# Storing the output of a linear attention in pairs of octets instead of octet by octet

## The chip, the cores and the metric

The kernel runs on one core of one Trainium2 chip. The metric is the device time of the execution in microseconds (us); lower is better. A run's profile spans from its first to its last instruction, and that span is 1.7 to 2.2 us shorter than the time. Each run also reports the mean clock granted to TensorE. With one core there is no second die to compare with, so a run is called slow if it lies over 1.5% above the fastest run of the same kernel; all comparisons here use fast runs.

## The reference

```python
# Q, K, V: float32, batch 8, heads 12, sequence 512, dim 64
Q_feat, K_feat = np.maximum(0, Q), np.maximum(0, K)
KV = np.einsum('bhkd,bhkv->bhdv', K_feat, V)
K_sum = np.sum(K_feat, axis=2)
numerator = np.einsum('bhqd,bhdv->bhqv', Q_feat, KV)
denominator = np.einsum('bhqd,bhd->bhq', Q_feat, K_sum)
return numerator / (denominator[:, :, :, None] + 1e-10)
```

96 heads of 512 x 64 are 12.58 MB for each of Q, K, V and the output. The kernel works on octets of 8 heads (twelve of them, numbered 0 to 11); K and V come in groups of 4 heads (24 groups, two to an octet).

## The kernel before

The parts that the change and the argument touch. All loads are issued at the start, as far as buffers are free, and cast to bf16 on the way; a store of octet `o` waits on SyncE's queue behind a copy of 128 bytes out of K of a group loaded well ahead, the "gate", so that stores go out in step with the loads.

```python
qin, kin, vin = pool("qin", 7), pool("kin", 12), pool("vin", 12)
outp = pool("outp", DELAY + 2)                  # DELAY = 5
# ... load_kv(g) loads K and V of a group, load_q(o) Q of an octet, all on GpSimd's queue
def denom(o):                                   # 16 matmuls, then VectorE on 128x256
    # ... ps = the denominators of all pairs (head of a row, head)
    nc.vector.scalar_tensor_tensor(own, ps, 1e-10, mask_h, op0=Alu.add, op1=Alu.mult)
    nc.vector.tensor_reduce(out=den, in_=own, op=Alu.add, axis=mybir.AxisListType.X)
    nc.vector.reciprocal(rec[o], den)
def norm(o, j, ps, o_sb):                       # half an octet: 128x1024 f32 out of PSUM
    rs = slice(16 * j, 16 * j + 16)
    nc.vector.tensor_tensor(o_sb[:, rs], ps, rec[o][:, rs]..., op=Alu.mult)
def store(o, o_sb):
    if o + DELAY < NO:                          # the gate
        nc.sync.dma_start(out=scratch, in_=k_sb[2 * (o + DELAY)][0:1, 0, :])
    # ... octet 11 in two halves of 4 KB rows, the others whole: 8 KB rows
    nc.sync.dma_start(out=Ov, in_=o_sb)
# ... the end of the program
norm(o, 1, ps, o_sb)                            # o = 10
store(o, o_sb)
idle(5, o + 1)                                  # matmuls into a bank that nobody reads
out_t(o + 1, (0,)); denom(o + 1); out_t(o + 1, (1,))
idle(6, o + 1)
backs(o + 1)                                    # transpose back, norm, twice; then two stores
```

## Time and profile before

| | before |
|---|---|
| time, median of 4 runs | 126.73 us (126.48 to 126.86) |
| span of the profiled run | 124.8 us |
| mean granted TensorE clock | 0.949 |
| HBM traffic | 37.75 MB read, 12.58 MB written |
| last load packet ends / last store packet ends | 110.0 / 123.6 us |

The views that carry the argument about what bounds this kernel are in the prediction. Two more of the kernel before are needed later. The first is a table by stage of the tail: of the numbers behind each stretch, the last three are the granted clock, the busy share of the DMA engines (small overlaps can bring it above 1) and the GB/s as written, in which a load counts with its two bytes per element.

```profile
core 0: us, PE busy (x) PEld busy (x) DVE busy (x) ACT busy (x) POOL busy (x), PEclk, DMA share, GB/s
...
107.00:108.50 1.50, 1.10 (x18) 1.09 (x18) 1.43 (x5) 1.12 (x2) 0.00 (x0) 1.00 1.06 350
108.50:119.00 10.50, 8.40 (x100) 7.29 (x97) 8.03 (x15) 4.64 (x9) 0.00 (x0) 1.00 1.01 418
119.00:121.00 2.00, 0.00 (x0) 0.00 (x0) 0.57 (x1) 0.00 (x0) 0.00 (x0) 1.00 0.98 410
...
123.50:124.90 1.40, 0.00 (x0) 0.00 (x0) 0.00 (x0) 0.00 (x0) 0.00 (x0) 0.50 0.00 0
```

The DMA share stays at 0.98 to 1.06 up to 121 us: the loads end and the stores go on with no gap. After 123.5 us nothing moves any more.

The second is the record of completions. The trace has sixteen increments of a DMA's semaphore for every store. I read them as one from each of the 16 engines, when its own share has landed, so that they show how far apart the engines are; the rate of the last part of the changed kernel, below, agrees with this reading. In the kernel before they are 1.55 to 1.65 us apart for every store from 110 us on. The last store's begin at 122.36, their mean is 123.22, and the sixteenth comes at 123.91 us.

### The profile page before, as it was taken

What the parts mean: (1) busy time and instruction counts of PE and PEld (TensorE: products, weight loads), DVE (VectorE), ACT (ScalarE), POOL (GpSimd) and SP (SyncE); (2) the same over time, 40 slices, a digit from 0 to 9 for tenths busy, and PEclk for the clock granted to TensorE, in tenths of its full rate; (3) what the DMA queues carried; (4) which work ended last, traced back from release to release, by engine and by line L of the source; (5) the groups of instructions that cost most, each with busy time, mean ns of one, the idle gap of its engine ahead of it and who ended that gap; (6) DMA issues with size and microseconds to landing.
All of it is one profiled execution on the core that took longest, in us unless ns stands there. A gap on an engine that the chain in (4) does not pass through costs nothing.

```text
span 124.8 us, 2656 instructions
## 1 busy us (share of the span) xinstructions
PE 86.6 (69%) x1067; PEld 78.5 (63%) x1067; DVE 81.1 (65%) x176; ACT 79.4 (64%) x114; POOL 31.2 (25%) x62
## 2 busy tenths in 40 slices
PE   0032287998889899893598599399777577797600
PEld 0031285997878787792597499299576476695500
DVE  2257644759797997989147845934928918979430
ACT  0163369989898999988149558665939737737100
POOL 6902434314243331142133115034122000000000
PEclk9999999999999999999779859959999999999995
DMA  3999999999999999999999999999999999999993
GB/s 112 377 306 215 215 205 210 217 205 218 203 215 211 206 223 324 253 216 300 281 215 280 304 213 249 331 215 230 334 234 218 323 257 215 312 421 420 428 416 143
DMA packets 10748, 32.68 MB, mean 262 GB/s; under 512 B 1392, under 2 KB 1392, under 8 KB 9328
## 3 DMA queue, kind: packets, MB, share of 16 engines
q0 software_dynamic: 8064, 17.83, 74.7%
q1 hardware_dynamic: 2384, 13.63, 27.1%
q10 hardware_dynamic: 288, 1.05, 2.2%
q8 instruction: 8, 0.13, 0.4%
q14 instruction: 4, 0.03, 0.1%
HBM read 37.75 MB, written 12.58 MB: 403 GB/s over the span
## 4 chain that ended last, share of the span: by engine, by line
DMA 34%; DVE 30%; PE 23%; ACT 5%; issue 2%; DVEq 1%; SPq 0%; POOLq 0%; ACTq 0%
DMA v_sb<-in_V_dram 14%; DVE o_sb L234 13%; DMA q_sb<-in_Q_dram 13%; PE ps_kv L150 11%; DMA kv_first<-in_K_dram 7%; PE ps_bk L228 7%; DVE kf L136 5%; PE ps_qt L171 4%; DVE vo L138 3%; ACT kvd L160 2%; DVE vo L145 2%; PE ps_ot L201 2%; DVE den L218 2%; ACT qt L179 2%; DVE rec L222 1%
## 5 line engine op out<-in xcount | busy, mean ns | idle before, releaser
L150 PE MATMUL ps_kv<-vo,kf 128*128 128x132 bf16 x384 | 30.8, 244 | 17.7 <-ACT vo L143 8.2
L150 PEld LDWEIGHTS <-kf 128*128 128x128 bf16 x384 | 28.4, 110 | 19.0 <-DVE vo L138 10.9
L234 DVE TENSOR_TENSOR o_sb<-ps_bk,rec 128x1024 f32<-128x1024 f32 x24 | 28.3, 1219 | 17.1 <-PE ps_bk L228 17.1
L160 ACT CAST kvd<-ps_kv 64x260 bf16<-64x260 f32 (+1 forms) x54 | 18.7, 346 | 19.5 <-PE ps_kv L150 16.6
L203 ACT COPY ot_sb<-ps_ot 128x1024 f32<-128x1024 f32 x24 | 24.0, 1014 | 3.0 <-PE ps_ot L201 2.0
L179 ACT ACTIVATE qt<-ps_qt 128x1024 bf16<-128x1024 bf16 x23 | 22.4, 1026 | 5.6 <-PE ps_qt L171 5.5
L228 PE MATMUL ps_bk<-ident,ot_sb 128*128 128x128 f32 x192 | 23.0, 273 | 0.4 <-ACT ot_sb L203 0.4
L136 DVE TENSOR_SCALAR kf<-k_sb,mask 128x1024 bf16<-128x1024 bf16 x44 | 18.4, 460 | 6.4 <-DMA k_sb<-in_K_dram 6.3
L94 POOL DMA_DIRECT2D k_sb<-in_K_dram x22 | 11.9, 542 | 37.7 <-DMA q_sb<-in_Q_dram 24.1
L228 PEld LDWEIGHTS ps_bk<-ident,ot_sb 128*128 128x128 f32 x192 | 20.8, 141 | 0.7 <-ACT ot_sb L203 0.7
L171 PE MATMUL ps_qt<-ident,q_sb 128*128 128x128 bf16 x192 | 16.0, 250 | 6.0 <-DMA q_sb<-in_Q_dram 5.9
L171 PEld LDWEIGHTS <-q_sb 128*128 128x128 bf16 x192 | 14.3, 114 | 7.3 <-DMA q_sb<-in_Q_dram 7.1
L201 PE MATMUL ps_ot<-qt,kvd 128*128 128x256 bf16 x96 | 14.7, 283 | 5.0 <-DVE o_sb L234 4.3
L96 POOL DMA_DIRECT2D v_sb<-in_V_dram x22 | 12.3, 558 | 17.4 <-DMA k_sb<-in_K_dram 11.1
L201 PEld LDWEIGHTS <-kvd 128*128 128x128 bf16 x96 | 9.2, 101 | 7.8 <-issue 5.7
L138 DVE TENSOR_SCALAR vo<-v_sb,mask 128x1024 bf16<-128x1024 bf16 x22 | 10.6, 482 | 1.8 <-DMA v_sb<-in_V_dram 1.8
L143 ACT ACTIVATE vo<-v_sb,mask 128x1024 bf16<-128x1024 bf16 x10 | 11.5, 1152 | 0.2
L210 PEld LDWEIGHTS <-qt 128*128 128x128 bf16 x192 | 6.8, 97 | 4.4 <-ACT qt L179 3.4
L210 PE MATMUL ps_den<-kvd,qt 128*128 128x16 bf16 x192 | 7.5, 180 | 2.4 <-ACT qt L179 2.1
L100 POOL DMA_DIRECT2D q_sb<-in_Q_dram x12 | 6.6, 546 | 8.5 <-DMA v_sb<-in_V_dram 6.2
L213 DVE SCALAR_TENSOR_TENSOR own<-ps_den,mask_h 128x256 f32<-128x256 f32 x12 | 5.0, 417 | 3.3 <-PE ps_den L210 3.3
L136 DVE TENSOR_SCALAR kf<-kv_first,mask 128x1024 bf16<-128x1024 f32 x4 | 2.8, 749 | 5.1 <-DMA kv_first<-in_K_dram 5.1
(24 smaller groups left out, 28.3 us busy)
## 6 DMA issues: line engine op xcount, KB each, us to landing
out_dram<-o_sb SPq DMA_DIRECT2D x11, 1024.0 KB, 9.0
q_sb<-in_Q_dram POOLq DMA_DIRECT2D x12, 512.0 KB, 14.8
k_sb<-in_K_dram POOLq DMA_DIRECT2D x22, 256.0 KB, 14.1
v_sb<-in_V_dram POOLq DMA_DIRECT2D x22, 256.0 KB, 13.2
kv_first<-in_V_dram ACTq DMA_DIRECT2D x2, 512.0 KB, 7.2
kv_first<-in_K_dram SPq DMA_DIRECT2D x2, 512.0 KB, 6.9
out_dram<-o_sb SPq DMA_DIRECT2D x2, 512.0 KB, 4.3
scratch<-k_sb SPq DMA_DIRECT2D x7, 0.1 KB, 5.0
```

The lines of the kernel that those rows point to most:

```text
L96: nc.gpsimd.dma_start(out=v_sb[g].rearrange("p r d -> p (r d)"), in_=Vr[g])
L136: nc.vector.tensor_scalar(kf[g][:, :, s, :], k_sb[g], scalar1=0.0, scalar2=mask[:, 0, s:s + 1], op0=Alu.max, op1=Alu.mult)
L138: nc.vector.tensor_scalar(vo[g % NB][:, :, 0, 2:D + 2], v_sb[g], scalar1=mask[:, 1, 0:1], scalar2=None, op0=Alu.mult)
L150: nc.tensor.matmul(ps_kv[:, g % 2, 0:2 * (D + 2)].rearrange("p (t d) -> p t d", t=2), kf[g][:, r, :, :].rearrange("p s d -> p (s d)"), vo[ ...
L160: copy(kvd[o % NK][64 * c:64 * c + 64, 4 * gs.start + s:4 * gs.stop:2, c * D1:c * D1 + D1].rearrange("p (g t) d -> p g t d", t=2), ps_kv[6 ...
L171: nc.tensor.transpose(ps[:, u, :], q_sb[o][:, i * (U // 2) + u, :], ident)
L179: nc.scalar.activation(to, ps, Act.Relu)
L201: nc.tensor.matmul(ps[:, i], kvd[o % NK][:, h, 1:2 * D + 1], q[:, :, h, :], start=True, stop=True, skip_group_check=True)
L203: nc.scalar.copy(ot[o][:, :, 4 * j:4 * j + 4], ps.rearrange("p h u c -> p u h c"))
L210: nc.tensor.matmul(ps[:, u], qt_sb[o % NZ][:, u, :], kvd[o % NK][:, :, 0:2 * D1:2 * D1 - 1], start=True, stop=True, skip_group_check=True)
L228: nc.tensor.transpose(ps[:, 2 * v:2 * v + 2].rearrange("p c d -> p (c d)"), ot[o][:, 8 * j + v].rearrange("p h c -> p (h c)"), ident32)
L234: nc.vector.tensor_tensor(o_sb[:, rs], ps, rec[o][:, rs].unsqueeze(2).to_broadcast([P, 16, D]), op=Alu.mult)
```

## The change

The first eight octets are stored in pairs: four stores of 2.1 MB with rows of 16 KB instead of eight of 1.05 MB with 8 KB. To bring a pair's rows together, Q of the two octets is interleaved before the transposes back, and the denominators of a pair are formed on 128x512 at a time. Pairs lag one pair behind. The last four octets go octet by octet as before. Three gates remain of seven, and the fourth pair's is on V of the last group: that store is to wait until all of K and V is in. Load buffers shrink to pay for larger output tiles.

```diff
-    qin = pool("qin", 7)
-    kin = pool("kin", 12)
-    vin = pool("vin", 12)
+    qin = pool("qin", 6)
+    kin = pool("kin", 9)
+    vin = pool("vin", 9)
-    outp = pool("outp", DELAY + 2)
+    outp = pool("outp", 3)
# ... kvd, qt_sb, ps_den, rec hold a pair; denom(o, x, n) works on n = 16 or 8 heads
-    def store(o, o_sb):
-        if o + DELAY < NO:
-            nc.sync.dma_start(out=scratch, in_=k_sb[2 * (o + DELAY)][0:1, 0, :])
+    def store(a):
+        gate = (None, k_sb[14], k_sb[18], v_sb[23])[a]
+        if gate is not None:
+            nc.sync.dma_start(out=scratch, in_=gate[0:1, 0, :])
+        nc.sync.dma_start(out=Or2[a], in_=o_sb[a].rearrange("p r d -> p (r d)"))
# ... octets 0 to 7 paired; then, L = 8:
+    a = L // 2
+    kvs(L)
+    prep(2 * L + 2)
+    prep_v(2 * L + 2, nc.scalar)
+    backs(a - 1, (0, 1))
+    octet(L)
+    prep(2 * L + 3)
+    prep_v(2 * L + 3, nc.vector)
+    kvs(L + 1)
+    backs(a - 1, (2, 3))
+    store(a - 1)
+    qt(L + 1)
+    backs(a, (0, 1))
+    store_octet(L, 1)
# ... octets 9, 10, 11 in the order of before
```

## The prediction

> **What bounds the kernel now.** I read the page's slices and DMA queues first, then windows of single phases, then the stores' issues on SyncE's queue, then VectorE's timeline over the last octets. (An octet is 8 heads: 3.15 MB read, 1.05 MB written; there are twelve.)
>
> ```profile
> DMA  3999999999999999999999999999999999999993
> GB/s 112 377 306 215 215 205 210 217 205 218 203 215 211 206 223 324 253 216 300 281 215 280 304 213 249 331 215 230 334 234 218 323 257 215 312 421 420 428 416 143
> ...
> q0 software_dynamic: 8064, 17.83, 74.7%
> q1 hardware_dynamic: 2384, 13.63, 27.1%
> ...
> HBM read 37.75 MB, written 12.58 MB: 403 GB/s over the span
> ```
>
> The DMA row is full from the second slice to the last but one. Q0 carries the casting loads (17.83 MB landed in bf16, so twice that leaves HBM), q1 the stores and half of the first loads.
>
> ```profile
> core 0: us, PE busy (x) PEld busy (x) DVE busy (x) ACT busy (x) POOL busy (x), PEclk, DMA share, GB/s
> 21.00:42.00 21.00, 19.35 (x262) 17.95 (x261) 16.94 (x35) 18.88 (x27) 7.21 (x14) 1.00 1.10 211
> 47.30:51.00 3.70, 3.14 (x40) 2.50 (x39) 3.18 (x5) 3.50 (x7) 0.43 (x1) 1.00 1.03 338
> 103.00:107.00 4.00, 2.89 (x36) 2.29 (x35) 3.59 (x6) 3.00 (x4) 0.00 (x0) 1.00 1.13 216
> 110.00:119.00 9.00, 6.90 (x86) 5.79 (x84) 6.53 (x11) 3.59 (x5) 0.00 (x0) 1.00 1.01 423
> ```
>
> The last column counts bytes as written. With loads alone (21 to 42 us) 211 GB/s is 422 GB/s at HBM; stores alone (110 to 119) move 423. In a mix (47.3 to 51) 338 written means, if loads plus stores still make about 418 at HBM, 258 of stores and 160 of loads: a store takes almost two thirds while it runs. So one number serves all phases: 50.33 MB at 421 GB/s is 119.5 us; with about 2 us before the first data and 3 us for the last ramp and the end, that is the 124.8 us span. The measured time is 1.9 us above the span. Compute may be late by any amount that leaves DMA work queued, and no more.
>
> ```profile
> 42.90 0.59 SPq L242 DMA_DIRECT2D scratch<-k_sb  x1
> 43.53 0.57 SPq L249 DMA_DIRECT2D out_dram<-o_sb  x1
> ...
> 102.85 0.50 SPq L242 DMA_DIRECT2D scratch<-k_sb  x1
> 103.45 11.23 SPq L249 DMA_DIRECT2D out_dram<-o_sb  x5
> 118.47 1.46 SPq L247 DMA_DIRECT2D out_dram<-o_sb  x2
> ```
>
> A store is issued as its gate, a load four to five octets ahead, has landed: one every 10 us. From 103.45 on the stores come ungated; the last two halves of the last octet are issued at 118.5 and 119.6 (the two in the last line) and land 4.3 us later. In the packet records stores run without a gap through this; at 119.6 some 0.4 to 0.9 MB of older stores was still ahead of the last half. That is 1 to 2 us of slack: compute that ends later than that shows in the time.
>
> ```profile
> 86.23 2.35 DVE L234 TENSOR_TENSOR o_sb<-ps_bk,rec 128x1024 f32<-128x1024 f32 x2 [1.57 <-PE ps_bk L228]
> ...
> 90.77 0.48 DVE L145 TENSOR_SCALAR vo<-v_sb,mask 128x1024 bf16<-128x1024 bf16 x1
> 94.23 2.36 DVE L234 TENSOR_TENSOR o_sb<-ps_bk,rec 128x1024 f32<-128x1024 f32 x2 [2.97 <-PE ps_bk L228]
> ...
> 99.96 0.48 DVE L145 TENSOR_SCALAR vo<-v_sb,mask 128x1024 bf16<-128x1024 bf16 x1
> 103.41 2.35 DVE L234 TENSOR_TENSOR o_sb<-ps_bk,rec 128x1024 f32<-128x1024 f32 x2 [2.97 <-PE ps_bk L228]
> 105.69 0.48 DVE L136 TENSOR_SCALAR kf<-k_sb,mask 128x1024 bf16<-128x1024 bf16 x1
> ```
>
> This is the compute that ends last. Per octet VectorE waits for TensorE's transposes back (2.97 us twice), normalises (2.35 us), and prepares two groups. From 86.2 to 105.7 there is no wait for a load: the chain VectorE, TensorE, VectorE sets the pace, 9.2 us an octet. From preparing group 22 (105.69) to the last half's issue (119.6) it is 13.9 us.
>
> **What the Trainium skill says.** "DMA: Bandwidth & Descriptors", Bandwidth, gives a fabric ceiling of 435 GB/s and 425 measured for 16 MB; the 421 to 423 above agree, so at most some 3% is left whatever the row size. Its Rules for kernel authors ask for 1 MiB or more per DMA; the stores have that already. In Queues, rings and completion order it says that an engine goes round-robin between queues at packet granularity; the two-thirds share of the 8 KB store rows beside loads agrees in kind, and would let 16 KB rows take at least as much. "VectorE: DVE Perf Modes", Why PSUM operands drop a tier, caps fp32 from PSUM at 1x; the normalisation (1219 ns for 1024 elements) and the masked add (417 ns for 256) agree: 1.04 ns for each further element.
>
> **The change part by part.**
>
> *Bytes and packets.* The bytes are the same. Stores go from 13 to 9 and gate copies from 7 to 3. A completion packet takes some 20 ns on an engine and a gate's 8-byte packet 36 ns (packet records), so 4 x 20 + 4 x (36 + 20) = 0.3 us at best. An 8 KB store packet takes 317 ns (25.8 bytes per ns), a 4 KB one mostly 159 (also 25.8): no fixed cost per row is visible, so 16 KB rows should bring nothing. Sum: 0 to -0.3 us on the floor.
>
> *Load buffers 12 to 9, Q 7 to 6.* A load is issued about 14 us before it lands, and compute is at most two octets behind; 9 buffers are 4.5 octets, above 33 us. No stall: 0.
>
> *VectorE per pair.* The paired denominators run twice per pair on 128x512 instead of 128x256: the masked add 417 + 256 x 1.04 = 0.68 us, the reduction likewise 0.69. Per pair + 4 x 0.27 = 1.1 us. Work per octet goes from 6.9 to 7.5 us, but it is uneven: an even octet has two preparations and two normalisations (about 6.1 us with the wait for TensorE), an odd one has the same plus 2 x (0.68 + 0.69 + 0.35), and waits for denominators and transposes in turn: about 10.7 us. At the start the two clears of kvd are twice as long and two more reductions are made (2 x 0.49 + 2 x 0.28 = 1.5 us), while octet 0 loses its denominators (1.2 us). A pair is then some 16.8 us against 14.2 (7.1 an octet between 26.3 and 40.7 us). DMA gives a pair 15 us in the load-only phase and 20 with stores. So compute, in step with the loads before, becomes 2 to 4 us late around 48 us and recovers partly: I place the start of octet 8 at 83 to 85 us, where before it was held by q_sb to 80.8 and by the preparation to 82.
>
> *Pair stores.* 2.1 MB at two thirds to four fifths of the bandwidth is 6.3 to 7.5 us in which loads crawl, against 4 us for one octet. Q of octets 5, 7 and 9 lands 1 to 2.5 us later; the even octets' land as before. About 1 us of this joins the lateness, the rest hides.
>
> *The tail.* The fourth pair's four normalisations come in octets 8 and 9's time, because pairs run one behind: between the start of octet 8 and group 22 VectorE now has eight normalisations, where it had six. Two more are 2.44 us, with TensorE's 16 transposes (1.9 us) between them, on the chain of the last fence. By hand, in the program's order on each engine and with the durations above: second half of octet 8's preparation 84.8; transposes and normalisations of pair 3 to 89.4; denominators 90.6; preparation 92.2; rest of pair 3 to 96.75; octet 8's own to 99.7; preparation, denominators, preparation to 103.7; octet 9's normalisations 106.7 to 109.0. Group 22 is prepared at 107.5 to 109.5 instead of 105.7: +2 to +4 us. From there on the program is as before, so the last half is issued at about 122.5.
>
> *The reserve.* At the last V's landing (before: about 106.6; after: about the same) there wait q_sb of octet 11 and 6.3 MB of stores: 7.3 MB, 17.5 us, to 123.7. That would cover a chain that ends by about 121. At 122.5 the queue has run dry or nearly: the last half then needs about 3.5 us (latency, 1.25 us of data, completion) instead of 4.3. Sum: +3.0 (chain) - 0.8 (no queue) - 0.3 (fewer packets) = +1.9 us: 128.6.
>
> **The rivals.** First, DMA stays the bound: full reserve, compute ends in time, 126.2 to 126.9. For it speaks that the DMA row is full in every slice and the gate on the last V is meant for just this. Against it: only 1 to 2 us of slack, and two normalisations more on a chain without load waits. Second, the odd octets run longer than I think, or the pair stores starve the loads at four fifths: chain +5 to +6, 130.5 to 131.5. For it: every odd octet has five handovers between TensorE and VectorE; against it: from octet 4 on DMA leaves 20 us a pair, in which 18 would still fit. Third, 16 KB rows or fewer changes between reads and writes raise the rate: mixed phases at 418 against 423 leave 1% of 30 us, 0.3 us; the equal rate of 4 and 8 KB packets speaks against more. 126.0.
>
> **Range and chances.** DMA-bound 126.3 and chain-bound 128 to 130.5 make a lopsided range, 126.2 to 130.8. The 2% line is 129.27, that is +2.5 us, inside the likely spread of the chain (+1 to +4.5 after the queue's slack): slower 0.38. Faster would need 124.2, below what 50.33 MB at the ceiling of 435 GB/s allow with the same start and end (115.7 + 5 + 1.9 = 122.6 at a perfect rate, never seen here): 0.03.
>
> **What would show it.** The store-only rate stays 420 to 427 GB/s and 16 KB packets take about 635 ns; if they take less than 610, the third rival has something. VectorE's masked add at 128x512 shows 0.65 to 0.72 us; odd octets are 3 to 5 us longer than even ones. Q of octet 7 lands later than 70.8, that of octet 8 not. Group 22's preparation starts after 107; the last store is issued after 121, and the DMA row has a hole or a thin slice just before the end. If instead the last issue is before 121 and the DMA row is full to the end, the chain's lateness was absorbed and the time is within 0.5 us of before.

## The result and the profile after

The time is 128.07 us (median of 4 runs, 127.96 to 128.17) against 126.73. All ratios here are the mean time of one kernel's fast runs over the mean of the other's of the same rounds, so not quite the ratio of the medians quoted. This one is 1.0108, with a 95% interval of 1.009 to 1.0126: 1.1% slower, within the 2%. The span grew from 124.8 to 126.3 us, and the granted clock rose from 0.949 to 0.979.

Of the page of the changed kernel, the slices' DMA share and GB/s, the stores' queue q1, the larger of two queues of kind "instruction", and the rate:

```profile
DMA  3999999999999999999999999999999999999981
GB/s 100 384 309 210 217 204 211 212 209 220 202 216 210 206 215 337 389 238 214 211 213 350 388 225 215 209 208 309 364 294 212 212 208 204 370 423 407 425 354 40
...
q1 hardware_dynamic: 1680, 13.63, 26.3%
...
q8 instruction: 8, 0.13, 0.4%
...
HBM read 37.75 MB, written 12.58 MB: 398 GB/s over the span
```

The DMA row is full up to the end, as before, except that the end is longer: the last two slices show 8 and 1, with 354 and 40 GB/s. Such a row hides a short gap in the middle of a slice. The table by stage, with the stretches used for before, shows it:

```profile
107.00:108.50 1.50, 1.01 (x13) 0.76 (x10) 1.50 (x5) 0.83 (x1) 0.00 (x0) 1.00 0.83 254
108.50:119.00 10.50, 8.88 (x111) 8.01 (x111) 7.96 (x18) 5.74 (x11) 0.00 (x0) 1.00 1.00 416
119.00:121.00 2.00, 0.62 (x6) 0.38 (x4) 2.00 (x2) 0.00 (x0) 0.00 (x0) 1.00 0.79 328
...
123.50:124.90 1.40, 0.00 (x0) 0.00 (x0) 0.00 (x0) 0.00 (x0) 0.00 (x0) 0.83 0.06 23
```

There are three differences. Between 107.0 and 108.5 us the DMA share falls to 0.83 (before 1.06): a hole where the loads end. Between 119 and 121 it is 0.79 (before 0.98): a dry spot just before the last halves are issued. And after 123.5 us, where before nothing moved, 23 GB/s still do. In the packet records the hole costs 0.5 us of the average engine's time and the dry spot 0.3 to 0.4 us.

SyncE's queue shows where the hole comes from:

```profile
82.68 0.50 SPq L276 DMA_DIRECT2D scratch<-k_sb  x1
83.28 0.53 SPq L277 DMA_DIRECT2D out_dram<-o_sb  x1
106.31 0.50 SPq L276 DMA_DIRECT2D scratch<-v_sb  x1
106.90 0.65 SPq L277 DMA_DIRECT2D out_dram<-o_sb  x1
107.65 13.85 SPq L283 DMA_DIRECT2D out_dram<-o_sb  x5
```

The fourth pair's store hangs on the gate of the last V. That V lands at 106.3 us, the gate copy is issued then, the store behind it at 106.90, and its first data moves at 108.05 (packet records). Meanwhile only Q of octet 11 is left to load, and it ends on the first engine at 107.3 and on the last at 108.8 us. An engine that has finished has nothing to do until 108.05.

The tail of the DMA work is best seen in fifths of a microsecond. These are the GB/s from 119 to 127 us, of the kernel before and of the changed one:

```profile
GB/s 492 369 410 451 389 389 430 410 430 328 410 471 369 430 430 348 287 266 287 164 184 102 21 0 0 0 0 0 0 0 0 0 0 0 0 0 0 0 0 0
```

```profile
GB/s 246 614 328 369 532 410 328 123 0 328 451 369 430 410 328 492 389 389 389 471 389 389 82 20 20 20 41 20 20 0 0 0 0 0 0 0 0 0 41 0
```

Before, the rate falls off over 1.5 us, because the engines are that far apart. After, it stands at about 400 until 123.4 and then at 20 for 1.2 us: one engine of sixteen (421 / 16 is 26 GB/s) is alone. The completions say the same. For the last store, fifteen increments come between 123.79 and 123.95 us, and the sixteenth at 125.22.

VectorE's timeline answers to the compute shown of before:

```profile
86.05 2.35 DVE L263 TENSOR_TENSOR o_sb<-ps_bk,rec 128x1024 f32<-128x1024 f32 x2 [0.89 <-PE ps_bk L255]
...
93.15 2.35 DVE L263 TENSOR_TENSOR o_sb<-ps_bk,rec 128x1024 f32<-128x1024 f32 x2 [2.08 <-PE ps_bk L255]
95.79 2.35 DVE L263 TENSOR_TENSOR o_sb<-ps_bk,rec 128x1024 f32<-128x1024 f32 x2 [0.29 <-PE ps_bk L255]
...
104.97 2.35 DVE L263 TENSOR_TENSOR o_sb<-ps_bk,rec 128x1024 f32<-128x1024 f32 x2 [2.97 <-PE ps_bk L255]
107.25 0.87 DVE L142 TENSOR_SCALAR kf<-k_sb,mask 128x1024 bf16<-128x1024 bf16 x2
...
118.78 2.36 DVE L263 TENSOR_TENSOR o_sb<-ps_bk,rec 128x1024 f32<-128x1024 f32 x2 [1.64 <-PE ps_bk L255]
```

The eight normalisations between the start of octet 8 and group 22 are the first four of these lines, two in each. Group 22's preparation begins at 107.25 (before 105.69), and the last pair of normalisations at 118.78 (before 117.22): the compute is 1.56 us later.

### Where the sixteenth engine's lag comes from

Besides loads, stores and gates, the packet records have a few packets of the instruction queues. Q8 has eight packets of 16 KB in a run, each 0.89 to 0.97 us long, and from the first to the last one comes on average after every 257 (before) or 262 (after) instructions of TensorE: TensorE is fetching its program. A single packet can only be on one of the sixteen DMA engines; the records don't say on which. The Trainium skill, "Runtime: NRT & Kernel Launch", Instruction fetch mechanics, describes just this: the instruction memory is refilled in 16 KiB blocks of 256 instructions over a DMA queue, and the cost of a crossing is "mostly hidden". Size and distance agree with the trace; whether it is hidden is the question here. Four stores' sixteen completions, as time of the first and the lag of the second-last and the last behind it, with TensorE's last fetch at 111.7 us (before) and 114.6 us (after):

| | before: first, 15th, 16th | after: first, 15th, 16th |
|---|---|---|
| store that completes just before the fetch | 110.07, +1.47, +1.55 | 113.33, +0.29, +0.39 |
| the next | 112.51, +1.56, +1.64 | 115.81, +0.41, +2.11 |
| the last but one (first half of octet 11) | 121.13, +1.54, +1.55 | 122.48, +0.19, +1.52 |
| the last | 122.36, +1.53, +1.55 | 123.79, +0.16, +1.43 |

In the changed kernel the hole lines the engines up, since those that are ahead wait for the store and those behind do not; then, within the store that follows the fetch, one of them falls 1.7 us behind the fifteenth, more than the 0.9 us of the fetch's own packet, and it is still 1.3 us behind the fifteenth at the end. Before, the engines were 1.6 us apart already, and the fetch made no difference to the last of them. That is an observation on two traces; the experiments test it.

### The profile page after: what moved, and what is told of

Same layout as the page of the kernel before. It is cut to its first block, busy times and chain, and to the rows that moved or that the text cites. A ratio compares the mean times of both kernels' runs of the same rounds, so it can differ in the third digit from the quotient of the medians.

```text
span 126.3 us, 2613 instructions
## 1 busy us (share of the span) xinstructions
PE 82.8 (66%) x1067; PEld 75.5 (60%) x1067; DVE 86.4 (68%) x178; ACT 79.2 (63%) x114; POOL 31.9 (25%) x62
## 3 DMA queue, kind: packets, MB, share of 16 engines
q10 hardware_dynamic: 288, 1.05, 2.1%
## 4 chain that ended last, share of the span: by engine, by line
DVE 33%; PE 26%; DMA 20%; ACT 12%; issue 3%; DVEq 1%; SPq 0%; ACTq 0%
DVE o_sb L263 15%; DMA v_sb<-in_V_dram 13%; PE ps_kv L156 10%; PE ps_bk L255 9%; DMA kv_first<-in_K_dram 7%; DVE kf L142 4%; ACT kvd L167 4%; ACT qt L191 4%; PE ps_qt L178 3%; ACT ot_sb L222 3%; DVE den L244 3%; DVE own L236 2%; DVE vo L144 2%; PE ps_ot L220 2%; PE ps_den L232 2%
## 5 line engine op out<-in xcount | busy, mean ns | idle before, releaser
L156 PE MATMUL ps_kv<-vo,kf 128*128 128x132 bf16 x384 | 27.9, 232 | 21.7 <-ACT vo L149 8.2
L156 PEld LDWEIGHTS <-kf 128*128 128x128 bf16 x384 | 25.6, 103 | 22.8 <-DVE vo L144 10.8
L255 PE MATMUL ps_bk<-ident,ot_sb 128*128 128x128 f32 x192 | 23.6, 274 | 0.5 <-ACT ot_sb L222 0.5
L178 PE MATMUL ps_qt<-ident,q_sb 128*128 128x128 bf16 x192 | 14.2, 233 | 1.8 <-DMA q_sb<-in_Q_dram 1.8
L178 PEld LDWEIGHTS <-q_sb 128*128 128x128 bf16 x192 | 13.0, 106 | 2.6 <-DMA q_sb<-in_Q_dram 2.3
L232 PE MATMUL ps_den<-kvd,qt 128*128 128x32 bf16 (+1 forms) x192 | 8.7, 195 | 5.4 <-ACT kvd L167 4.5
L232 PEld LDWEIGHTS <-qt 128*128 128x128 bf16 x192 | 8.1, 100 | 6.8 <-issue 5.7
L236 DVE SCALAR_TENSOR_TENSOR own<-ps_den,mask_h 128x512 f32<-128x512 f32 (+1 forms) x12 | 6.9, 579 | 6.7 <-PE ps_den L232 6.7
L103 POOL DMA_DIRECT2D q_sb<-in_Q_dram x12 | 7.2, 601 | 8.2 <-DMA v_sb<-in_V_dram 4.5
L244 DVE TENSOR_REDUCE den<-own 128x32 f32<-128x512 f32 (+1 forms) x12 | 7.1, 595 | 0.3
```

The lines of the kernel that those rows point to most:

```text
L156: nc.tensor.matmul(ps_kv[:, g % 2, 0:2 * (D + 2)].rearrange("p (t d) -> p t d", t=2), kf[g][:, r, :, :].rearrange("p s d -> p (s d)"), vo[ ...
L178: nc.tensor.transpose(ps[:, u, :], q_sb[o][:, i * (U // 2) + u, :], ident)
L232: nc.tensor.matmul(ps[:, u], qt_sb[a % NZ][:, x * U + u, :], kvd[a % NK][:, h0:h0 + n, 0:2 * D1:2 * D1 - 1], start=True, stop=True, skip_g ...
L255: nc.tensor.transpose(ps[:, 2 * v:2 * v + 2].rearrange("p c d -> p (c d)"), ot[a][:, 8 * j + v], ident32)
```

## The experiments

Two theories of the +1.34 us: *the chain* (compute that ends later, as predicted; then moving the gate changes nothing, and more delay costs its full size) and *the gate* (the hole behind the last V; then undoing the gate alone brings the time back, with compute as late as it is; the texts call this the queue theory, and the straggler theory where the lagging engine is meant). For the second, it is also open whether the hole itself or the lagging engine makes the loss. Twelve kernels ran, each beside 11 runs of the kernel before on the same chip (medians 126.71 to 126.81).

**1 and 2. One and two more normalisations on the chain (changed kernel).** The second half of octet 9 is normalised two or three times, each 1.22 us of VectorE.

```diff
-    backs(a, (2, 3))
+    backs(a, (2,))
+    backs(a, (3,), 1)        # and 2: the normalisation once and twice more, same result
     store_octet(L + 1, 1)
```

> The changed kernel with octet 9's last normalisation done twice: the chain on VectorE becomes 1.2 us longer, the stores and bytes stay. Chain theory (as in the prediction: the end is set by VectorE's chain, 1.56 us later than before): 128.07 + 1.2 = 129.3 us. Queue theory (the end is set by the one of 16 DMA engines that is 1.3 us behind the others through all the last stores, because an instruction fetch of 0.93 us fell on it after a hole had lined the engines up): the other 15 engines take up the 1.2 us, 128.1 to 128.4 us.

> The same with the normalisation done three times, chain 2.4 us longer. Chain theory: 130.5 us. Queue theory: the 15 engines now end last, 2.4 us after the last issue: 129.2 to 129.5 us, that is a rise of 1.2 and not of 2.4.

Measured 130.29 us (128.88 to 130.49, 6 runs, ratio 1.0264, 1.0227 to 1.03) and 130.77 (130.66 to 131.46, 5 runs, 1.0336, 1.0313 to 1.0358). The first is more than either theory had, because more than 1.22 us was added. In its profiled run (129.93) the last pair of normalisations starts 2.36 us later than in the changed kernel (121.14 against 118.78), and nearly half of that arises at 81.7 us, far ahead of the edit. TensorE's groups there, of the changed kernel and of experiment 1, with the idle time ahead of them in brackets:

```profile
81.45 1.07 PE L178 MATMUL ps_qt<-ident,q_sb 128*128 128x128 bf16 x16 [0.98 <-DMA q_sb<-in_Q_dram]
82.36 1.11 PE L156 MATMUL ps_kv<-vo,kf 128*128 128x132 bf16 x16
```

```profile
81.68 1.65 PE L178 MATMUL ps_qt<-ident,q_sb 128*128 128x128 bf16 x16 [0.99 <-DMA q_sb<-in_Q_dram]
83.13 3.05 PE L156 MATMUL ps_kv<-vo,kf 128*128 128x132 bf16 x31
```

The same 16 transposes take 1.07 us in one and 1.65 in the other, after the same idle time of 1 us, and the granted clock over these stretches is 1.00 and 0.61. The kernel before has such a slow stretch there too (0.61 from 80.8 to 85.2 us). It comes and goes between runs of one kernel: the run of 128.88 us fits a chain without it. The Trainium skill, "TensorE: Matmul & The Clock Gate", Part 1, has a cold state at half clock after an idle window of about 3.4 us; here waits of 1.0 to 2.5 us came before such a stretch in some runs, and in the changed kernel none followed a wait of 1.0 us. So a delay of this kernel's compute is uncertain by 1.1 us in itself. What follows for the theories: in the changed kernel the end does follow a chain that is made later still. The fifteenth completion of the last store moves by the same 2.36 us (126.31 against 123.95), the run's time by 1.8, since the sixteenth is now 0.94 us behind instead of 1.27. That lag isn't the old one: in the store before it, the sixteen completions are within 0.18 us, and a packet of the other instruction queue falls at 125.5. In experiment 2's profiled run (130.69) the last pair starts 4.05 us later than in the changed kernel, not 2.44; the fifteenth completion moves by 4.01 (127.96), the sixteenth comes 0.03 us behind it, and the time moves by 2.6. So no slack is left there, but that doesn't make the chain the cause of the first 1.34 us.

**3. The gate of the fourth pair on the last K (changed kernel).**

```diff
-        gate = (None, k_sb[14], k_sb[18], v_sb[23])[a]
+        gate = (None, k_sb[14], k_sb[18], k_sb[23])[a]
```

> The changed kernel with the fourth pair's store gated on the last K instead of the last V, 1.2 us earlier. Queue theory: the hole between the last load and the fourth pair's store (rate down to 200 GB/s, 0.5 us lost per engine) closes; 127.5 to 127.7 us, and the engines stay spread. Chain theory: the chain is not touched, 128.0 to 128.2 us.

Measured 126.89 us (126.57 to 127.74, 6 runs), ratio 1.0031 (1.0002 to 1.0059). One word brings back 1.2 of the 1.34 us. The tail by stage, and its GB/s from 119 to 127 us:

```profile
107.00:108.50 1.50, 0.85 (x8) 0.60 (x7) 1.50 (x5) 1.00 (x2) 0.00 (x0) 1.00 1.09 388
...
119.00:121.00 2.00, 0.45 (x5) 0.21 (x2) 1.97 (x2) 0.00 (x0) 0.00 (x0) 1.00 0.55 227
...
123.50:124.90 1.40, 0.00 (x0) 0.00 (x0) 0.00 (x0) 0.00 (x0) 0.00 (x0) 0.50 0.00 0
GB/s 451 246 246 328 82 164 123 0 307 328 492 369 410 389 451 369 430 389 451 369 451 82 0 0 0 0 0 0 0 0 0 41 0 0 0 0 0 0 0 0
```

The hole is gone (1.09) although the compute is as late as in the changed kernel: the last pair of normalisations starts at 118.61 (118.78 there). The dry spot is deeper (0.55), since the same bytes went out earlier. It costs nothing: the last store ends at 123.90 us, as before (123.91), and its sixteen completions lie within 0.3 us. They were 2.0 us apart before the dry spot, so there the engine that lagged caught up. Two of the six runs took 127.74 us; they have no profile, and why is not known.

**4. The gate on K of group 22, where the kernel before has it (changed kernel).**

```diff
-        gate = (None, k_sb[14], k_sb[18], v_sb[23])[a]
+        gate = (None, k_sb[14], k_sb[18], k_sb[22])[a]
```

> The changed kernel with the fourth pair's gate on the K of group 22 (3.7 us before the last V), which is what the kernel before had for octet 6. Queue theory: no hole, 126.6 to 127.0 us as with the last K; the last V and Q land later because the store takes four fifths of the bandwidth beside them, so perhaps 0.5 us more if VectorE waits for them. Chain theory: 128.0 us.

Measured 126.85 us (126.64 to 128.28, 6 runs), ratio 1.0023 (0.9989 to 1.0057). Still earlier brings no more. There is no hole; the completions of the last store lie within 0.2 us, the last of them at 123.94. The last pair of normalisations starts at 118.8, just as in the changed kernel.

**5. The gate on the last V in the kernel before.** Octet 6's store, which is the seventh, is gated on the last V; nothing else changes.

```diff
-            nc.sync.dma_start(out=scratch, in_=k_sb[2 * (o + DELAY)][0:1, 0, :])
+            gate = v_sb[23] if o == 6 else k_sb[2 * (o + DELAY)]
+            nc.sync.dma_start(out=scratch, in_=gate[0:1, 0, :])
```

> The kernel before with one edit: the store of octet 6 (and so all after it) waits for the last V instead of group 22's K. Nothing of the compute changes. Queue theory: the same hole after the last load (0.5 us) and the same straggler after the fetch at 111.7 as in the changed kernel, 127.4 to 128.2 us. Chain theory (only VectorE's order costs time): 126.5 to 126.9 us, as before.

Measured 128.27 us (128.06 to 128.32, 5 runs), ratio 1.0108 (1.0092 to 1.0125): the ratio of the whole change, from its gate alone. Stage and tail:

```profile
107.00:108.50 1.50, 0.51 (x5) 0.31 (x4) 1.50 (x5) 1.44 (x2) 0.00 (x0) 1.00 0.70 158
...
123.50:124.90 1.40, 0.00 (x0) 0.00 (x0) 0.00 (x0) 0.00 (x0) 0.00 (x0) 0.79 0.14 53
GB/s 573 287 451 532 246 532 369 369 532 307 307 451 430 369 492 348 389 410 430 410 389 430 205 62 61 61 41 20 41 20 20 0 0 0 0 0 0 0 0 0
```

The hole is there (0.70), and so is the long foot at 20 to 60 GB/s after 123.4 us. In this profiled run the compute was 1.1 us later than in the kernel before (last pair of normalisations at 118.3), because TensorE's clock fell to 0.82 between 95 and 104.5 us (1.00 before). It did not set the end: with the hole, the stores were later still, and there is no dry spot (share 1.01 between 119 and 121 us). Experiments 3 to 5 together settle the first question: the loss is the gate's. With the gate undone all the rest of the change, the chain's lateness included, is worth 0.15 us by the medians, 0.2 to 0.3% by the ratios.

**6. The end of the chain in the kernel before.** One more normalisation of octet 9, to measure the slack.

```diff
         for j in range(2):
-            norm(o, j, back(o, j), o_sb)
+            ps = back(o, j)
+            norm(o, j, ps, o_sb)
+            if o == 9 and j == 1:
+                norm(o, j, ps, o_sb)
```

> The kernel before with octet 9's last normalisation done twice: VectorE's chain 1.2 us later, about as late as the change makes it (1.56), and nothing else. If the queue of stores takes this up, as the slack of 1 to 2 us in the prediction says: 126.7 to 127.0 us. If the chain sets the end of the kernel before: 127.9 us.

Measured 127.86 us (127.10 to 128.73, 6 runs), ratio 1.0084 (1.0049 to 1.0119). In its profiled run (127.14) the last pair of normalisations starts 2.1 us later than before (119.3 against 117.22), 1.2 from the edit and the rest from TensorE's clock, and the last completion comes 0.56 us later (124.47): some 1.5 us of the delay were swallowed. The median is nevertheless the one expected if the chain sets the end, so the slack did not cover most of the runs; of the other five only one (127.10) lies near the profiled one. The wide spread of its runs fits a chain that is bimodal by 1 us around the edge of the slack.

**7. The fourth pair's normalisations in VectorE's waits, with the early gate (changed kernel).** An attempt at a kernel better than both.

```diff
+    backs(a - 1, (2,))
     kvs(L + 1)
-    backs(a - 1, (2, 3))
-    store(a - 1)
     qt(L + 1)
     backs(a, (0, 1))
-    store_octet(L, 1)
# ... after prep_v(2 * L + 5, nc.vector); the gate is k_sb[23], as in 3:
+    backs(a - 1, (3,))
+    store(a - 1)
+    store_octet(L, 1)
```

> The changed kernel with the gate on the last K and with the second half of pair 3's normalisations moved into VectorE's two waits in octets 8 and 9 (2.1 and 3.0 us idle): chain about 1.5 us shorter, last issue at about 119.6. With the hole closed the engines ran dry before the last octet (0.9 us lost at 119 to 121), so here the chain should count: 125.6 to 126.4 us, below both kernels. If the chain has slack there: 126.9 us as with the gate alone.

Measured 127.09 us (126.74 to 128.66, 6 runs, one of them slow), ratio 1.0033 (0.9994 to 1.0073). The compute is 0.8 us earlier than in the changed kernel (118.0), but the last completion stays at 123.97, and the mean of the sixteen is 123.25 (before 123.22). So in this run an earlier chain brings nothing; that the bytes are then the limit is what is left, and was not tested further. No version beat the kernel before.

**8. The pair stores as two stores of 8 KB rows (changed kernel).**

```diff
-        nc.sync.dma_start(out=Or2[a], in_=o_sb[a].rearrange("p r d -> p (r d)"))
+        Ov = Or2[a].rearrange("p (r d) -> p r d", d=D)
+        for j in range(2):
+            nc.sync.dma_start(out=Ov[:, RQ * j:RQ * j + RQ], in_=o_sb[a][:, RQ * j:RQ * j + RQ])
```

> The changed kernel with each pair stored as two DMAs of 8 KB rows (at a pitch of 16 KB), the schedule else unchanged. If the row size does nothing, as predicted: 127.9 to 128.4 us, a store rate of 420 to 427 GB/s as with 16 KB rows, and loads keep about a third instead of a fifth of the bandwidth beside a store. If 16 KB rows save something: 0.3 us or more slower than the changed kernel.

Measured 128.74 us (128.42 to 128.96, 5 runs), ratio 1.015 (1.0129 to 1.017), 0.67 us above the changed kernel. The packets answer what rows are worth: a 16 KB packet takes 624 ns beside loads and 611 alone (medians), an 8 KB one 322 and 309, so per byte the longer row saves 3% in a mix and 1% alone. The share of the HBM traffic that a store takes beside loads (median over the quarter-microseconds in which it has over 0.3) is 0.81 with 16 KB rows and 0.67 with these, 0.64 in the kernel before. The time, however, isn't cleanly the rows': in the profiled run TensorE's slow clock made the chain 1.2 us later than in the changed kernel (120.0), and the dry spot is 1.1 us. What the row size alone does to the time stays open, within about 0.7 us.

**9 and 10. Where the fetch falls.** Idle matmuls early in the program move TensorE's place in its stream, and with it the fetches.

```diff
     for g in range(2, NB):
         zero(g)
+    for _ in range(75):      # changed kernel; 62 in the kernel before with the gate of 5
+        nc.tensor.matmul(..., ident, ident, start=True, stop=True, skip_group_check=True)
     mm_kv(0)
```

> The changed kernel with 75 idle matmuls in TensorE's first wait (150 more instructions), so that the last instruction fetch on the DMA engines, at 114.6 us, comes about 6 us earlier, before or in the hole after the last load. Queue theory: no engine is 1.3 us behind in the last stores any more; the end comes when the 15 ended, 126.9 to 127.4 us. Chain theory: 128.0 to 128.2 us. If it is the number of bytes on that engine and not the time of the fetch, also 128.0.

> The kernel before with the gate on the last V (128.27 us) and 62 idle matmuls in TensorE's first wait: 124 more instructions, so that the last 16 KB fetch of TensorE instructions moves from 112.2 to about 106.5 us, ahead of the hole, and (unlike the try with 150) no ninth fetch follows. Straggler theory: the engine that fetches catches up in the hole, the 16 completions of the last store lie within 0.8 us, 127.0 to 127.6 us. If the hole alone makes the loss: 128.2 us.

Measured 128.31 us (128.10 to 128.57, 4 runs, 1.0126, 1.0111 to 1.0142) and 128.41 (128.30 to 129.28, 6 runs, 1.0144, 1.012 to 1.0169). Neither got faster, so both expectations of the fetch theory were missed. In both the eighth fetch moved ahead of the hole as meant (106.2 and 105.7 us), but the added instructions brought a ninth, at 118.6 and 119.4. The spread of completions in the second, store by store, is 0.54, 0.50, 0.45 and 0.62 us up to 119 us, with no straggler; after the ninth fetch it is 2.07, 2.01 and 1.94. So the fetch does make the lag, and within the store that follows it. What the lag is worth in time these two do not say.

**11. Fewer matmuls, so fewer fetches (changed kernel; wrong result).** Half of the matmuls that form KtV are left out in octets 0 to 3.

```diff
-        for r in range(R):
+        for r in range(R if g >= 8 else R // 2):
```

> The changed kernel with half of the key-value matmuls of octets 0 to 3 left out: a wrong result there on purpose, 128 TensorE instructions fewer, so that the last 16 KB fetch of TensorE instructions falls to about 106 us, before the hole, and none falls into the last stores. The changes of compute lie where DMA sets the pace. Queue theory with the straggler (one engine 1.3 us behind because of the fetch at 114.6 sets the end at 124.8, while the other 15 end at 123.6): 126.8 to 127.1 us, and the 16 completions of the last store within 0.4 us. If the hole after the last V alone costs the time: 128.0 us. Chain theory: 128.0 us.

Measured 129.57 us (128.51 to 131.36, 6 runs, two of them slow), ratio of the fast ones 1.0179 (1.0144 to 1.0214). It failed as an experiment: the chain ended 2.5 us later (121.3; the granted clock was 0.953, in the changed kernel 0.979), and a fetch came at 122.4 us anyway.

**12. The gate of 5, with the last fetch ahead of the hole and none after it (wrong result in octet 11).** 68 idle matmuls early, and half of the KtV matmuls of groups 22 and 23 left out to keep the ninth fetch away.

```diff
+    for _ in range(68):
+        nc.tensor.matmul(ps_den[:, 1, 0:128], ident, ident, start=True, stop=True, skip_group_check=True)
# ... in mm_kv:
-        for r in range(R):
+        n = R // 2 if g >= 22 else R
+        for r in range(n):
```

> The kernel before with the gate on the last V, 68 idle matmuls early, and half of the matmuls that form KtV left out in groups 22 and 23 (a wrong result in the last octet, on purpose), so that TensorE's last instruction fetch should come at about 105.5 us of the span and no ninth in the store phase. If the straggling engine is made by a fetch after the hole, and the end waits for that engine: 126.9 to 127.3 us, the sixteen completions of the last store within 0.6 us of each other, and the last store packet at about 123.6 us. If the hole alone makes the loss (or the gate does so through anything else): 128.2 us, like the same gate without these edits, with the completions close together but all of them late.

Measured 127.81 us (127.29 to 128.26, 6 runs), ratio 1.0071 (1.0046 to 1.0097), between the two expectations and inside neither, though its fastest run touches the first. The fetch came at 105.0 and no other of TensorE's before the end of the stores. Completions are 0.18 to 0.34 us apart from 111 to 121.5 us: no straggler, as the fetch theory says. The end of the profiled run, which was its slowest:

```profile
GB/s 655 410 246 655 246 410 614 164 532 492 164 430 410 389 389 430 410 389 389 451 410 348 389 348 21 20 20 41 0 0 0 0 0 0 0 0 0 0 0 0
```

A foot at 20 GB/s is there again, shorter: an 8 KB packet of the other instruction queue, q14 (0.31 us), falls at 122.8, and the last two stores' sixteenth completions come 0.63 and 1.08 us behind the first. The kernel before has such a packet at 122.6 too, where it changes nothing. The summary of the last store:

| kernel | mean of 16 | 15th | 16th | median time |
|---|---|---|---|---|
| before | 123.22 | 123.89 | 123.91 | 126.73 |
| changed | 123.94 | 123.95 | 125.22 | 128.07 |
| 3: gate on the last K | 123.69 | 123.78 | 123.90 | 126.89 |
| 5: before, gate on the last V | 124.14 | 124.95 | 125.59 | 128.27 |
| 12: 5 without TensorE's late fetch | 124.26 | 124.28 | 125.18 | 127.81 |

The sixteenth completion goes with the time: the profiled run takes 2.7 to 2.9 us more than it in the first four rows, 3.1 in the last. In the changed kernel the mean engine is 0.72 us later than before, more than the 0.5 us of the hole, but the other fifteen engines end only 0.04 us later than before's last; the remaining 1.27 us are the sixteenth alone. In 5 and 12, which differ by the fetch and by a hole of 0.54 and 0.66 us, removing TensorE's straggler gave 0.46 us of the median, not the 1.0 to 1.4 that I expected; in the profiled run a second, smaller straggler and a slightly larger hole stand in the place of the rest. What the others of its six runs did isn't recorded.

One more reading of the completions separates the chain from the lagging engine. From the issue of the last half to its fifteenth completion it takes 4.29 us in the kernel before, where older stores are still queued, but 2.78 in the changed kernel and 2.75 to 2.79 in experiments 1 to 4, 6, 8, 9 and 11, which all have a dry spot: there the queue is empty, and fifteen engines end when the chain lets them. So the slack of the kernel before is 1.5 us, and the changed chain, whose last half is issued 1.57 us later (121.17 against 119.60), just uses it up. The hole adds nothing to the end of these fifteen: the dry spot is 0.5 us shallower with it (0.3 to 0.4 us of the average engine's time in the changed kernel, 0.8 in experiments 3 and 4). What it does, by this reading, is to line up the fifteen ahead of the sixteenth, and to leave that one too little of a dry spot to catch up in. In 5 and 12 there is no dry spot (4.27 and 5.21 us from issue to fifteenth completion), so there the hole itself delays all engines; that 5 has the very ratio of the change is in part a coincidence.

## Why the prediction was right in size, and not in cause

128.07 us lies within the range 126.2 to 130.8, 0.5 us below the 128.6, and within 2% was the likeliest class. That the size came out was luck: the chain and the empty queue, put at +2.2 us together, come to +0.06, and 1.3 us of another cause, which the sum did not have, took their place. Step by step:

- *Bytes and packets*: right. 16 KB packets take 624 and 611 ns (expected about 635), nothing that the time could show.
- *Load buffers*: right. Between 45 and 106 us the rate at HBM falls short of 421 GB/s by 0.66 us in sum, before by 0.84; no loads were starved.
- *VectorE per pair*: right in its terms:

```profile
L244 DVE TENSOR_REDUCE den<-own 128x32 f32<-128x512 f32 x8 | 5.5, 682 | 0.2
L236 DVE SCALAR_TENSOR_TENSOR own<-ps_den,mask_h 128x512 f32<-128x512 f32 x8 | 5.3, 658 | 6.7 <-PE ps_den L232 6.7
```

  682 and 658 ns for the predicted 0.69 and 0.68 us. From preparation to preparation octets 2 and 4 take 6.3 and 6.2 us (6.1 predicted), 3 and 5 take 10.5 and 10.4 (10.7 predicted), octet 7 takes 8.7.
- *Pair stores*: right. The share is 0.81, "four fifths"; Q of octet 7 landed at 71.6 us, later than the 70.7 of before. One miss: Q of octet 8, which was not to be later, landed at 81.4 us (80.7 before).
- *The tail*: the order was right, the size was half. The ends of work that the prediction named came earlier by a growing amount: pair 3's first normalisations at 88.4 (89.4), the rest of pair 3 at 95.5 (96.75), octet 8's own at 98.1 (99.7), octet 9's at 107.3 (109.0). One us is lost at the first, where I let VectorE wait 2.2 us for the transposes and it waited 0.89. Group 22 starts at 107.25: +1.56, under the +2 to +4. The stretch from there to the last issue is as of before, 13.9 us, and the last half is issued at about 121.2 instead of 122.5.
- *The reserve*: here the prediction failed. It set q_sb of octet 11 and 6.3 MB of stores waiting at the last V's landing, let the queue run on, and summed +3.0 (chain) - 0.8 (no queue) - 0.3 (fewer packets). (Its own 106.6 and 17.5 us give 124.1 for the end of the queue, not 123.7; nothing hangs on that.) The queue did run nearly dry, but the first two terms were mis-sized: the chain is 1.57 us later at the last issue, and without a queue the last half needs 1.51 us less (2.78 against 4.29). Together they are +0.06 us, not +2.2, and with the gate on an earlier K such a chain costs 0.15 us of the median (experiments 3 and 4). What cost was left out of the sum: the stores were *waiting behind the gate*, not queued at the engines. From the landing of the last V (106.3) to the first store data (108.05) are 1.75 us, and behind that V there is only 1.05 MB of Q to fill them. The hole that this makes leaves one engine 1.27 us behind the fifteen others at the end.
- The first rival leaned on the same mistake ("the gate on the last V is meant for just this"). "A hole or a thin slice just before the end" did come (the dry spot), but it is not what cost.

What is shown: the gate on the last V, alone, makes the loss of the whole change (1.0108 and 1.0108), and taking it away alone removes all but 0.2% to 0.3%. What is seen in the completions of every run with this gate: the hole lines the engines up, and an instruction fetch behind it leaves one engine late, until a long enough dry spot lets it catch up (experiments 1 and 2). In the changed kernel's profile that one engine is the whole loss; that this holds for its other runs is not shown, and no run has the changed kernel with the hole and without a fetch behind it. What stays open is also how much the hole and the fetch share in experiment 5.

## What to carry to other kernels

A gate that holds stores back until the last load has landed gives up the DMA engines for as long as an issue takes to reach them; open it one load earlier, so that something is left to move in between. When the end of a kernel is one long stream of stores, look at the sixteen completions of the last one before looking at compute: the end is set by the last engine, and what ran on a single engine behind the last wait stayed in the time here unless a later dry spot let that engine catch up (experiments 1 to 4). A prediction that sums reserves must ask of each transfer whether it is already in a queue or still behind a wait.

## What the Trainium skill lacked or had wrong

- "Runtime: NRT & Kernel Launch", Instruction fetch mechanics, has the cost of crossing a 16 KiB block "mostly hidden". It isn't told there what the block takes from the kernel's own transfers: here a packet of 0.9 us for TensorE's 16 KB, after which one engine was 1.3 to 1.7 us behind the others until the end of a stream of stores; an 8 KB block of another queue (0.31 us) went with a lag of 0.9 us.
- "DMA: Bandwidth & Descriptors", Queues, rings and completion order, gives the rule of turns between queues. The split that follows between a casting load and a store isn't there: beside the same loads a store took 0.64 to 0.67 of the HBM traffic with 8 KB rows and 0.81 with 16 KB rows.
- No page says that a wait for all of the loads lines the engines up: the completions of one store were 1.6 us apart in a continuous stream and 0.2 to 0.4 after the hole.
- "TensorE: Matmul & The Clock Gate", Part 1, has half clock after an idle window of about 3.4 us. Here half clock (0.61 on average over 4.4 us) followed waits of 1.0, 1.5 and 2.5 us, and full clock another wait of 1.0 us. The same part also tells of a kernel whose clock swings with short idles between groups of matmuls, but gives no length for them.
